# A hybrid RWKV-7, GLA and RetNet trunk: TensorE's order in the mixers taken from a model of the other engines' queues

## The chip, the cores and the metric

The kernel runs on one core of a Trainium2 chip. The metric is the device time of one execution in microseconds (us). Three runs of the kernel before took 3447.75, 3429.0 and 3440.02 us, a median of 3440.02. TensorE (PE in the profile) multiplies matrices, VectorE (DVE) and ScalarE (ACT) work on what it leaves in PSUM, GpSimd (POOL) works on SBUF, and SyncE (SP) issues most transfers. Each engine takes its instructions strictly in the order of the program and waits where an operand isn't ready.

## The reference

The reference is one inference step of two layers over 1024 new prompt tokens and 8 sample sequences of 4 tokens, width 1024, in float32. Each layer projects its input, runs three kinds of heads on parts of the projection, projects their output back, and applies a gated feed-forward network (FFN) with a short convolution:

```python
for l in range(DEPTH):
    p = x @ w_in[l]
    p_rw, p_gl, p_rt = _split(p, (RWKV_COLS, GLA_COLS, RET_COLS))
    y_a, sh, s_a = _rwkv7_mix(p_rw, ...)     # 6 heads
    y_b, s_b = _gla_mix(p_gl, ...)           # 5 heads
    y_c, s_c = _ret_mix(p_rt, s_ret[l], pos) # 5 heads
    mix = jnp.concatenate([y_a, y_b, y_c], axis=-1) @ w_out[l]
    x = _layer_norm(ALPHA * x + mix, ln1_g[l], ln1_b[l])
    f, cv = _conv_ffn(x, s_conv[l], ffn_up[l], ...)
    x = _layer_norm(ALPHA * x + f, ln2_g[l], ln2_b[l])

def step(s, inp):                            # RWKV-7, for each token
    r_t, w_t, a_t, b_t, k_t, v_t = inp
    sa = jnp.einsum('bhvk,bhk->bhv', s, a_t)
    s = s * w_t[:, :, None, :] + sa[..., None] * b_t[:, :, None, :] + v_t[..., None] * k_t[:, :, None, :]
    return s, jnp.einsum('bhvk,bhk->bhv', s, r_t)
```

GLA and RetNet are computed in chunks of 64 tokens with a state of their own. All final states are outputs too.

## The kernel before, in words

Large products keep float32 accuracy by splitting each operand into a high and a low part: `mm3` issues three matmuls, high times high, low times high and high times low. Their tiles are named `pa` (RWKV's part of the projection, channels by tokens), `gt` (the rest of the projection, tokens by channels), `po` (output projection), `pu` and `pd` (FFN). Weights come from DRAM by SyncE, and ScalarE (`wih`) and GpSimd or VectorE (`wil`) split them (L188).

The mixers of a layer run in two stages. In the first, RWKV works on nine batches, eight of 128 prompt tokens (two chunks of 64) and one of the samples. Of a batch, `rwkv_front` (L473) makes the operands with VectorE, ScalarE and GpSimd from two small products `zw` and `za`, up to `ra` and `bk` (L533); `rwkv_gram` (L537) multiplies them to gram matrices (`gps`, masked into `gm` at L559); `rwkv_solve` (L599) sends those through DRAM, solves a triangular system by pairs of VectorE instructions (L630, L632), and sends the result back. `rwkv_merge` (L647) joins the halves by the small products `xps`, `tps` and `ups`, each of which needs ScalarE's copy of the one before (L656, L661, L666); `rwkv_gate` makes the output gate (`gp`), in the same PSUM bank. `rwkv_core` (L678) runs one chunk: products with the state (`zy<-st`) and with the values (`zy<-sav`), ScalarE's copy `zs` (L688), the product `sp`, the copy `sav` (L693), the state update `up` with VectorE's L720, and the last products into `zy`, copied to `ys` (L698). In the second stage GLA (`gtp`, `gsp`, `gop`, `gup`) and RetNet (`rtp`, `rsp`, `rop`, `rup`) go through nine token tiles; `finish` (L979) normalizes a tile with a reduction (L985), a reciprocal root by Newton steps of tiny VectorE instructions (tiles `nw`, L242 to L248) and two products (L989, L990) into `yt`. `yrows` transposes `yt` (`ytp`), and `out_proj` multiplies by the output weights and adds the residual (`ac`, L1325) ahead of the layer norm (L940).

What sets TensorE's order is a small scheduler that runs while the program is written. Each part is a generator (`Stream`, L75) that emits a burst of instructions and then yields a time in us, an event or a condition. `Tensor.run` (L142) always steps the first stream whose time has come; the projection `gt` and `pa` serve as filler when no chain step is ready. `Tensor.order` (L111) adds to the clock `max(0.025, cols*passes/2400)` us for each matmul and chains every matmul to its predecessor, so TensorE keeps exactly this order. How long a step waits for its answer comes from the table `AFTER` (L35) of fixed delays, one number per kind of step. `TE.post` (L133) puts off a store or another action by such a number. The other engines' instructions stand in the order in which the streams emit them, as the tile framework places them.

Of the kernel before, what the change touches and what calls it, by code (L numbers as in the profile page):

```python
# [34 lines left out]
# expected times (us) from a step to what it makes ready  # L35
AFTER = {"key": 5.93, "sh": 3.5, "rkv": 2.0, "block": 6.0, "blockin": 2.5, "x": 3.0, "operands": 8.0, "gram": 0.9, "tv": 0.9, "tb": 0.9, "solve": 24.0, "ud": 4.5, "joined": 4.0, "mask": 1.5, "gd": 4.5, "x11": 1.28, "x21": 1.4, "x22": 0.6, "z": 1.4, "s": 1.58, "am": 2.0, "sx": 1.0, "sout": 3.0, "y": 7.3, "gate": 1.4, "state": 2.5, "done": 7.0, "turn": 2.5, "tokin": 3.36, "ev": 2.25, "gexp": 2.6, "gqt": 1.6, "rrot": 5.5, "rqt": 2.0, "at": 2.5, "qm": 0.8, "vx": 0.9, "gstate": 1.2, "tk": 4.5, "gateout": 4.0, "yin": 2.2, "yout": 4.5, "gnext": 1.2, "rout": 8, "rnext": 0.8, "yt": 0.5, "yready": 1.79, "ln": 3.0, "lnk": 1.5, "lns": 3.0, "ln1": 3.0, "ln2": 9.0}
# [18 lines left out]
# constant columns  # L55
# [9 lines left out]

class Event:
    """A time on the tensor engine from which something it has to wait for is expected."""

    def set(self, after=0.0):
        self.time = Event.clock() + after  # L70
# [4 lines left out]
class Stream:  # L75
    """Work on the tensor engine in bursts: yields the time (us) until the next one can start, or an Event or a condition."""
# [13 lines left out]
    def step(self, clock):  # L90
        x = next(self.gen, self)
        if x is self:
            return False
        if isinstance(x, (int, float)):
            self.ready = clock() + x
        else:
            self.wait = x
        return True


class Tensor:
    """The tensor engine, its instructions kept in the order of the program, with an estimate of its time (us)."""

    def __init__(self, tc, engine):
        self.tc, self.engine, self.t, self.last, self.posts = tc, engine, 0.0, None, []
# [5 lines left out]
    def order(self, ins, cols, passes):  # L111
# [5 lines left out]
        self.t += max(0.025, cols * passes / 2400)  # L117
# [1558 lines left out]
```

## Time and profile before

| | us |
|---|---|
| median of three runs | 3440.02 |
| span of the profiled execution (the page gives no other time of it) | 3430.9 |
| mixers of layer 0 | 0 to 929 |
| FFN of layer 0 | 929 to about 1718 |
| mixers of layer 1 | about 1718 to 2645 |
| FFN of layer 1 | 2645 to 3431 |

The profile has 22110 matmul instructions on TensorE, 5037 instructions on VectorE, 3208 on ScalarE and 1660 on GpSimd. The boundaries of the stages are read from the first `pu` and the first `pa` of the layers. In the waits of the profile a row names the engine and line that waits, the one waited for, then the sum, the number of times and the longest wait. Beside the busy times stands the clock that TensorE was granted, as a share of its full one.

### The profile page before, as it was taken

The page shows a single profiled execution, that of the slowest core. Times are in us where ns is not written, and L with a number is a line of the kernel's source. Part 1 is how long each engine was busy: PE and PEld are TensorE (multiplying, and loading weights), DVE is VectorE, ACT ScalarE, POOL GpSimd, SP SyncE. Part 2 cuts the span into 40 slices and gives each one's busy share as a digit, 9 for nine tenths or more (in the row PEclk, how much of TensorE's full clock was granted, in tenths as well). Part 3 has the DMA queues.
Part 4 walks back from the last instruction along what each step waited for, and adds up shares of the span by engine and source line. Part 5 has one row for each costly group of instructions (what it writes and reads, how often), then busy time and mean ns, then how long its engine had stood idle before and what let it go on. Part 6 is the DMA issues. An engine that isn't in the chain of part 4 may idle for free.

```text
span 3430.9 us, 59397 instructions
## 1 busy us (share of the span) xinstructions
PE 3198.4 (93%) x22110; PEld 2975.9 (87%) x22110; DVE 2068.6 (60%) x5037; ACT 1434.7 (42%) x3208; POOL 1332.6 (39%) x1660
## 2 busy tenths in 40 slices
PE   9889999988899999999888999999788999999995
PEld 8778888776799999999877888887777999999995
DVE  3577565776756544454746866646777564545457
ACT  6554332334543334333575543323346423333335
POOL 5443222224553334333565522221336433433345
PEclk9789999998999999999998999999989999999998
DMA  7333213433311111111154432234433111111111
GB/s 249 112 110 99 79 54 102 139 115 102 106 60 47 44 44 50 50 44 50 56 164 140 133 91 68 63 128 119 129 94 100 48 44 44 56 44 44 44 44 56
DMA packets 233261, 288.24 MB, mean 84 GB/s; under 512 B 65212, under 2 KB 146908, under 8 KB 232972
## 3 DMA queue, kind: packets, MB, share of 16 engines
q1 hardware_dynamic: 223852, 271.98, 26.3%
q10 hardware_dynamic: 9120, 12.47, 1.2%
q8 instruction: 173, 2.83, 0.4%
q14 instruction: 116, 0.95, 0.1%
HBM read 225.94 MB, written 58.43 MB: 83 GB/s over the span
## 4 chain that ended last, share of the span: by engine, by line
PE 70%; DVE 16%; DMA 4%; ACT 4%; issue 3%; POOL 2%; SPq 1%; ACTq 0%; DVEq 0%; POOLq 0%
PE pu L128 27%; PE pd L128 13%; PE gt L128 9%; PE pa L128 5%; PE po L128 3%; DVE tm L630 2%; DVE U L632 2%; PE zy L128 2%; PE gps L128 2%; PE rop L128 1%; DVE c L1401 1%; PE gop L128 1%; POOL wil L188 1%; DMA N<-gd 1%; DVE s L940 1%
## 5 line engine op out<-in xcount | busy, mean ns | idle before, releaser
L1401 DVE SCALAR_TENSOR_TENSOR c<-u,ppt,c 128x32 f32<-128x32 f32 (+1 forms) x704 | 395.8, 589 | 545.5 <-ACT c L1392 523.8
L188 POOL TENSOR_TENSOR wil<-wir,wih 128x512 fp32r<-128x512 f32 (+1 forms) x264 | 366.3, 1395 | 365.8 <-ACT wih L188 361.2
L128 PE MATMUL gt<-wih,xh 128*128 128x320 f32 (+1 forms) x1008 | 340.1, 339 | 0.9 <-DVE mx L388 0.9
L1448 DVE TENSOR_TENSOR acc<-acc,pd 128x384 f32<-128x384 f32 (+1 forms) x480 | 247.7, 518 | 139.5 <-PE pd L128 137.5
L128 PE MATMUL gt<-wil,xh 128*128 128x320 f32 (+1 forms) x1008 | 316.1, 315 | 6.5 <-POOL wil L188 5.2
L128 PE MATMUL gt<-wih,xl 128*128 128x320 f32 x896 | 281.6, 314 | 0.0
L188 ACT CAST wih<-wir 128x512 fp32r<-128x512 f32 (+1 forms) x296 | 185.6, 637 | 162.4 <-PE po L128 71.5
L128 PE MATMUL pa<-xh,wih 128*128 128x384 f32 (+1 forms) x576 | 216.5, 376 | 20.4 <-DVE mx L388 11.8
L630 DVE TENSOR_TENSOR tm<-U,N 96x60 f32<-96x60 f32 (+24 forms) x558 | 179.1, 321 | 69.9 <-DMA N<-gd 48.4
L128 PEld LDWEIGHTS gt<-wih,xh 128*128 128x128 f32 (+1 forms) x1008 | 187.5, 186 | 38.6 <-issue 21.9
L128 PE MATMUL pa<-xl,wih 128*128 128x384 f32 (+1 forms) x576 | 201.4, 350 | 3.3 <-POOL xl L188 3.0
L128 PE MATMUL pa<-xh,wil 128*128 128x384 f32 (+1 forms) x576 | 200.7, 348 | 3.6 <-POOL wil L188 2.2
L128 PEld LDWEIGHTS gt<-wil,xh 128*128 128x128 f32 (+1 forms) x1008 | 188.5, 187 | 10.2 <-POOL wil L188 9.1
L188 POOL TENSOR_TENSOR hl<-c,hh 128x384 fp32r<-128x384 f32 x132 | 128.1, 971 | 159.6 <-ACT hh L188 133.0
L632 DVE TENSOR_TENSOR U<-U,tm 96x60 f32<-96x60 f32 (+24 forms) x558 | 170.3, 305 | 14.0
L128 PEld LDWEIGHTS gt<-wih,xl 128*128 128x128 f32 x896 | 173.1, 193 | 0.0
L1392 ACT ACTIVATE c<-pu,ppt 128x384 f32<-128x384 f32 (+1 forms) x264 | 172.8, 655 | 0.0
L1380 ACT COPY u<-pu 128x384 f32<-128x384 f32 x176 | 84.1, 478 | 195.2 <-PE pu L128 195.1
L188 ACT CAST hh<-c 128x384 fp32r<-128x384 f32 x132 | 64.4, 488 | 222.4 <-DVE c L1407 222.3
L128 PEld LDWEIGHTS pa<-xh,wih 128*128 128x128 f32 x576 | 119.7, 208 | 35.1 <-DVE mx L388 13.2
L128 PE MATMUL po<-yh,wih 128*128 128x384 f32 (+1 forms) x384 | 138.9, 362 | 9.1 <-DVE ac L1325 6.7
L128 PE MATMUL po<-yh,wil 128*128 128x384 f32 (+1 forms) x384 | 131.7, 343 | 3.7 <-DVE wil L188 3.7
(810 smaller groups left out, 9862.6 us busy)
## 6 DMA issues: line engine op xcount, KB each, us to landing
wir<-in_wA_dram SPq DMA_DIRECT2D x144, 256.0 KB
wir<-in_wO_dram SPq DMA_DIRECT2D x96, 256.0 KB
wir<-in_wB_dram SPq DMA_DIRECT2D x56, 320.0 KB
tokd<-ev SPq DMA_DIRECT2D x112, 160.0 KB
x<-rkvd SPq DMA_DIRECT2D x16, 576.0 KB
tk<-tokd SPq DMA_DIRECT2D x16, 480.0 KB
rkvd<-mx SPq DMA_DIRECT2D x36, 192.0 KB
tk<-tokd SPq DMA_DIRECT2D x16, 400.0 KB
```

The lines of the kernel that those rows point to most:

```text
L128: self.order(self.engine.matmul(out, lhsT, rhs, start=start, stop=stop), cols, 4 if rhs.dtype == F32 else 1)
L188: return A.copy(dst_h, src), (le or G).tensor_tensor(dst_l, src, dst_h.bitcast(F32), ALU.subtract)
L630: V.tensor_tensor(tm, U[:, 0:nr, i:i + 1].to_broadcast([4 * ns, nr, 31 - i]), N[:, i:i + 1, i + 1:32].to_broadcast([4 * ns, nr, 31 - i]), ...
L632: V.tensor_tensor(U[:, 0:nr, i + 1:32], U[:, 0:nr, i + 1:32], tm, ALU.add)
L940: self.ends["V"] = V.tensor_tensor(self.s1, acc[0] if k == 1 else self.s1, acc[k], ALU.add)
L1380: A.copy(u[:, 2:386], ps)
L1392: A.activation(c[:, :W], ps, AF.Identity, scale=pc(PP_CV + 4 * t + 2), bias=pc(PP_CV + 4 * t + 3))
L1401: V.scalar_tensor_tensor(cv, src, pc(PP_CV + 4 * t + tap), cv, ALU.mult, ALU.add)
L1448: V.tensor_tensor(acc[n][m], acc[n][m], ps, ALU.add)
```

## The change

The table `AFTER` goes, but for three constants. In its place a `Model` is kept while the program is written: a list of busy intervals for VectorE, ScalarE, GpSimd and SyncE's queue, the time at which each region of a tile is written and last read, and a single figure for the transfers' bus. Every instruction of those engines is wrapped (`Timed`): it is entered into its engine's list at the first gap from the time its operands and its buffer are ready, with a cost by its size. TensorE's clock is raised to the time at which the model has the operands of a matmul ready. `ready(x)` is the modelled time at which `x` can be read, and `slot(tag)` of a pool the time at which its next buffer is free. Every `yield AFTER[...]` becomes a yield of such times, and every post fires at such a time. The projection's steps also wait for their weights and for a free bank, in the model. The chain's `turn` delay is left out. What is computed and the number of instructions on each engine stay as they are, save ScalarE's table loads: the program has 71 where it had 65.

```diff
-AFTER = {"key": 5.93, ..., "x": 3.0, "operands": 8.0, "gram": 0.9, ..., "x11": 1.28, "x21": 1.4, "x22": 0.6, "z": 1.4, "s": 1.58, ..., "gate": 1.4, "state": 2.5, "done": 7.0, "turn": 2.5, ..., "yt": 0.5, "yready": 1.79, ...}
+PACE = {"x": 3.0, "start": 4.0, "lnk": 1.5}
...
+class Model:
+    TABLE = {AF.Exp: "e", AF.Tanh: "e", AF.Ln: "l", AF.Gelu_apprx_tanh: "g"}
...
+    def ready(self, *aps):
+        t = 0.0
+        for ap in aps:
+            n, r = self.box(ap)
+            t = max(t, self.latest(self.writes.get(n, {}), r))
+        return At(t)
...
+    def place(self, e, at, dur):
+        b = self.busy[e]
+        i = len(b)
+        while i > 1 and b[i - 1][0] >= at:
+            i -= 1
+        while True:
+            t = max(at, b[i - 1][1])
+            if i == len(b) or t + dur <= b[i][0]:
+                b.insert(i, (t, t + dur))
...
+    def cost(self, e, op, out, ins, func):
...
+        if e == "V":
...
+                o = m / 960 + 0.065
+            return o, o + 0.15
+        if e == "A":
+            o = m / 1200 + 0.055
+            return o, o + 0.15
...
+        o = m * 2.34 / 1000 + 0.06
+        return o, o + 0.1
...
-        self.t += max(0.025, cols * passes / 2400)
+        self.t = self.model.matmul(out, lhsT, rhs, self.t, dur) + dur
...
+        dur = 2 * max(0.03, cols * 2 / 2400 + 0.006) if rhs.dtype == F32 else cols / 2400 + 0.0135
...
             A.copy(x11[0:32], ps[0:32, :384])
-            yield AFTER["x11"]
+            yield ready(x11[0:32])
...
-            yield AFTER["x22"]
+            yield ready(s.sh[0], s.sh[1])
             rwkv_gate(s)
...
             A.copy(zs, zy[Cn:C2, :w])
-            yield AFTER["z"]
+            yield ready(zs)
...
             A.copy(savc[0:Cn], sp[:Cn, :w])
-            yield AFTER["s"]
+            yield ready(savc[0:Cn])
...
-                yield AFTER["gate"]
+                yield late(ready(s.gm, s.sav), 0.0 if s.smp else ready(sts[state_at[0]]), pz.slot("zy"))
...
                         if c:
-                            yield AFTER["state"]
+                            yield late(ready(sts[state_at[0]]), pz.slot("zy"))
...
-                s.done.set(AFTER["done"])
-                yield AFTER["turn"]
+                s.done.set()
...
-            yield AFTER["x"]
+            yield late(ready(s.sh[0]), pm.slot("m", ahead=2))
...
-            yield AFTER["operands"]
+            yield ready(s.ra, s.bk)
...
+                    yield late(pg.slot("g"), feed.at(2 * 3 * NA + 4 * gi, 0))
                     ps = pg.tile([P, 512], F32, tag="g", name="gt")
...
-                s.out.set(AFTER["rout"])
-                yield AFTER["rnext"]
+                s.out.set(ready(s.yt))
+                yield pn.slot("b", BB)
...
-                    yield AFTER["yt"]
+                    yield pg.slot("g")
                 if i % 3 == 2:
-                    yready[n].set(AFTER["yready"])
+                    yready[n].set(ready(*ys[n][:2]))
```

How the order moves is shown at three places. The rows have the line, the operation, the tile written and the tiles read, the shape, and how often a row repeats. All matmuls of the changed kernel carry the line of its helper, L322, and all its VectorE instructions that of the wrapper, L253.

First TensorE, layer 0, the merge and the first chunk of a batch in the middle of the stage. Before, from `ups` to the chunk's product with the state:

```order
L128 MATMUL ups<-gm,x_3579 32x32 x12
L128 MATMUL tv<-cs,v 128x128 x3
L128 MATMUL gp<-bgt,sh 128x384
L128 MATMUL gp<-bgt,sg 128x384
L131 MATMUL tb<-cs,bk 128x128 x4
L128 MATMUL gt<-wih_2999,xh_401 128x320
L128 MATMUL gt<-wil_2998,xh_401 128x320
L128 MATMUL gt<-wih_2999,xl_402 128x320
L128 MATMUL gt<-wih_2999,xh_401 128x320
L128 MATMUL gt<-wil_2998,xh_401 128x320
L128 MATMUL gt<-wih_2999,xl_402 128x320
L128 MATMUL zy<-st_165,ra 128x128 x3
```

and in the changed kernel, from `ups` to `sp`:

```order
L322 MATMUL ups<-gm,x_3847 32x32 x12
L322 MATMUL gp<-bgt,sh 128x384
L322 MATMUL gp<-bgt,sg 128x384
L322 MATMUL zy<-st_165,ra 128x128 x3
L322 MATMUL zy<-sav,gm 64x64 x6
L322 MATMUL gt<-wih_3616,xh_92 128x320
L322 MATMUL gt<-wil_3615,xh_92 128x320
L322 MATMUL gt<-wih_3616,xl_93 128x320
L322 MATMUL gt<-wih_3616,xh_92 128x320
L322 MATMUL gt<-wil_3615,xh_92 128x320
L322 MATMUL gt<-wih_3616,xl_93 128x320
L322 MATMUL sp<-zs,gm 64x64 x6
```

`gp` and `zy` follow `ups` directly, and six products of `gt` stand ahead of `sp`; `tv` and `tb` of another batch have moved elsewhere.

Second TensorE, layer 0, the gram matrices of the first batch. Before:

```order
L128 MATMUL gps<-ra,bk 128x128 x4
L128 MATMUL pa_1_1084<-xh_222,wih_1009 128x384
L128 MATMUL pa_1_1084<-xl_223,wih_1009 128x384
L128 MATMUL pa_1_1084<-xh_222,wil_1008 128x384
L128 MATMUL pa_1_1084<-xh_222,wih_1009 128x384
L128 MATMUL pa_1_1084<-xl_223,wih_1009 128x384
L128 MATMUL pa_1_1084<-xh_222,wil_1008 128x384
L128 MATMUL gps<-ra,bk 128x128 x4
```

and in the changed kernel:

```order
L322 MATMUL gps<-ra,bk 128x128 x8
L322 MATMUL pa_1_1238<-xh_172,wih_1149 128x384
L322 MATMUL pa_1_1238<-xl_173,wih_1149 128x384
L322 MATMUL pa_1_1238<-xh_172,wil_1148 128x384
L322 MATMUL gps<-ra,bk 128x128 x2
L322 MATMUL pa_1_1238<-xh_172,wih_1149 128x384
L322 MATMUL pa_1_1238<-xl_173,wih_1149 128x384
L322 MATMUL pa_1_1238<-xh_172,wil_1148 128x384
L322 MATMUL gps<-ra,bk 128x128 x2
L322 MATMUL tv<-cs,v 128x128 x3
```

Eight products of `gps` come in a row where two groups of four had six large products between them.

Third VectorE, layer 0, second stage, the end of a RetNet tile's normalization. Before (the `nw` with the higher numbers belong to GLA's tile, whose output is `yg`):

```order
L246 TENSOR_TENSOR nw_7867<-nw_7866 128x5
L248 SCALAR_TENSOR_TENSOR nw_7895<-nw_7896,nw_7895 128x5
L247 SCALAR_TENSOR_TENSOR nw_7867<-nw_7867,nw_7865 128x5
L1029 TENSOR_TENSOR tk<-tk,E 128x320
L246 TENSOR_TENSOR nw_7896<-nw_7895 128x5
L248 SCALAR_TENSOR_TENSOR nw_7866<-nw_7867,nw_7866 128x5
L247 SCALAR_TENSOR_TENSOR nw_7896<-nw_7896,nw_7894 128x5
L989 TENSOR_TENSOR yt<-yt,nw_7866 128x320
L248 SCALAR_TENSOR_TENSOR nw_7895<-nw_7896,nw_7895 128x5
L1089 TENSOR_TENSOR qm<-qT,cs 128x256
L990 SCALAR_TENSOR_TENSOR yt<-yt,gate 128x320
```

and in the changed kernel:

```order
L253 SCALAR_TENSOR_TENSOR nw_8106<-nw_8107,nw_8106 128x5
L253 TENSOR_TENSOR nw_8107<-nw_8106 128x5
L253 SCALAR_TENSOR_TENSOR nw_8107<-nw_8107,nw_8105 128x5
L253 SCALAR_TENSOR_TENSOR nw_8106<-nw_8107,nw_8106 128x5
L253 TENSOR_TENSOR nw_8107<-nw_8106 128x5
L253 SCALAR_TENSOR_TENSOR nw_8107<-nw_8107,nw_8105 128x5
L253 SCALAR_TENSOR_TENSOR nw_8106<-nw_8107,nw_8106 128x5
L253 TENSOR_TENSOR yt<-yt,nw_8106 128x320
L253 TENSOR_TENSOR yl_8185<-ytp,yh_8184 128x4x128
L253 SCALAR_TENSOR_TENSOR yt<-yt,gate 128x320
```

One normalization runs at a time: GLA's tiles have gone through theirs before RetNet's first `yt`.

More of the change, by code (lines that the diff above doesn't have):

```diff
@@ L64, with set @@
 NCS = _off
+class At(float):
+    pass
 class Event:
-    def set(self, after=0.0):
-        self.time = Event.clock() + after
+    def set(self, at=0.0):
+        self.time = max(Event.clock(), at)
     time = None
@@ new lines, with __init__, __getattr__, traced @@
+class Timed:
+    def __init__(self, model, engine, name):
+        self.model, self.engine, self.name = model, engine, name
+    def __getattr__(self, op):
+        call = getattr(self.engine, op)
+        def traced(*args, **kw):
+            ins = call(*args, **kw)
+            aps = [a for a in list(args) + list(kw.values()) if isinstance(a, bass.AP)]
+            func = next((a for a in args if isinstance(a, AF)), None)
+            self.model.add(self.name, op, ins, aps[0], aps[1:], func)
+            return ins
+        return traced
@@ new lines, with __init__, tile, slot @@
+class Pool:
+    def __init__(self, model, pool, bufs, since):
+        self.model, self.pool, self.bufs, self.since, self.tags = model, pool, bufs, since, {}
+    def tile(self, shape, dtype, tag=None, name=None, bufs=None, **kw):
+        key = tag or name
+        if tag is not None:
+            kw["tag"] = tag
+        if bufs is not None:
+            kw["bufs"] = bufs
+        t = self.pool.tile(shape, dtype, name=name, **kw)
+        n = t.tensor.name
+        h = self.tags.setdefault(key, [])
+        b = bufs or self.bufs
+        if len(h) >= b:
+            self.model.before[n] = h[-b]
+        elif self.since:
+            self.model.floor[n] = self.since
+        h.append(n)
+        return t
+    def slot(self, tag, bufs=None, ahead=1):
+        h, b = self.tags.get(tag, []), bufs or self.bufs
+        return At(max([self.model.idle(n) for n in h[len(h) - b:len(h) - b + ahead] if len(h) >= b] or [self.since]))
@@ L101, with late, __init__ @@
+def late(*times):
+    return At(max(times))
 class Tensor:
-    def __init__(self, tc, engine):
-        self.tc, self.engine, self.t, self.last, self.posts = tc, engine, 0.0, None, []
+    def __init__(self, tc, engine, model):
+        self.tc, self.engine, self.model, self.t, self.last, self.posts = tc, engine, model, 0.0, None, []
         Event.clock = self.clock
@@ L109, in clock, with order @@
         return self.t
-    def order(self, ins, cols, passes):
+    def order(self, ins, out, lhsT, rhs, dur):
         ins = ins.ins
@@ L270, in gemm_steps @@
     def gemm_steps(feed, first, xs, n, name, free):
+        yield late(pg.slot("g"), feed.at(first, 0), ready(xs[n][0][:, 0], xs[n][1][:, 0]))
         ps = pg.tile([P, 512], F32, tag="g", name=name)[:, :NB[n][1]]
@@ L274, in gemm_steps @@
         for k in range(KD):
+            if k:
+                yield late(feed.at(first, k), ready(xh[:, k], xl[:, k]))
             h, lo, end = feed.k(first, k)
@@ L568, in rwkv_tok @@
             s.vt = rp.tile([P, 384], F32, tag="vt", name="vt", bufs=2)[:W]
+            yield late(ready(s.v), pm.slot("m"))
             tv = pmt("tv")
@@ L1326, in out_proj @@
                 ln.add(m, V if n == 2 else G)
-            yield AFTER["ln"]
+            yield late(ready(ln.s1, ln.s2), pg.slot("g", ahead=2))
             ln.stats()
```

333 lines of the change are left out of this document (221 added, 112 removed).

## The prediction

> **What bounds the kernel now.** I read the page first, for the engine that sets the end, then busy time by stage, then TensorE's waits, then the granted clock in short windows.
>
> ```profile
> span 3430.9 us, 59397 instructions
> ...
> PE 70%; DVE 16%; DMA 4%; ACT 4%; issue 3%; POOL 2%; SPq 1%; ACTq 0%; DVEq 0%; POOLq 0%
> ```
>
> TensorE is the bound, with 70% of the chain that ended last, and VectorE is the only other engine with a large share of it. The same by stage (first column the stretch, then its length, then busy time and instructions of each engine; the decimal ahead of the last two numbers is TensorE's mean granted clock):
>
> ```profile
> 0.00:275.00 275.00, 242.48 (x1476) 218.64 (x1477) 156.55 (x423) 158.13 (x330) 135.63 (x158) 0.85 0.51 156
> 275.00:605.00 330.00, 317.09 (x2714) 277.97 (x2713) 198.72 (x745) 112.35 (x272) 82.65 (x80) 0.97 0.29 84
> 605.00:929.00 324.00, 277.39 (x2104) 234.05 (x2103) 239.16 (x561) 133.17 (x344) 115.71 (x95) 0.92 0.39 116
> ...
> 1718.00:1975.00 257.00, 226.73 (x1473) 202.76 (x1471) 160.97 (x451) 166.83 (x356) 144.45 (x166) 0.90 0.50 147
> 1975.00:2310.00 335.00, 319.67 (x2796) 280.18 (x2797) 206.08 (x758) 115.36 (x288) 85.16 (x85) 0.98 0.31 87
> 2310.00:2645.00 335.00, 287.60 (x2119) 245.84 (x2119) 241.82 (x570) 144.90 (x355) 121.06 (x107) 0.92 0.36 108
> ```
>
> The rows are the two layers' mixers, three stretches each; the FFNs, left out here, have the same order on TensorE in both programs. So the change can act on these 1856 us. Length less PE busy leaves 32.5, 12.9, 46.6, 30.3, 15.3 and 47.4, or 185 us, without work on TensorE. One minus the clock, times the length, gives 41, 10, 26, 26, 7 and 27, or 136 us, that the clock took. What TensorE waited for:
>
> ```profile
> PE ytp L131 <- DVE yt L990: 20.2, 10, 4.0
> PE ytp L131 <- DVE ac L1325: 18.0, 5, 7.2
> ...
> PE gps L128 <- DVE bk L533: 12.5, 5, 6.0
> ...
> PE zy L128 <- ACT ys L698: 4.2, 2, 2.4
> PE zy L128 <- DVE st L720: 3.2, 1, 3.2
> PE sp L128 <- ACT zs L688: 2.6, 3, 1.6
> PE up L128 <- ACT sav L693: 2.4, 2, 1.8
> PE gp L128 <- ACT gm L666: 1.8, 1, 1.8
> ```
>
> The last five rows are the handovers inside the RWKV chain: 14.2 us in all. The fixed delays cover the chain well already; the transposes of the mixers' output (ytp), 38.2 us, are the largest item.
>
> **The change, part by part.** The work is the same; its order on TensorE differs, and with it the cover, the work that lies between a product and the product that waits for another engine's answer.
>
> *The chain's steps.* Between two steps stood twelve products of gt or pa, now six, and between ups and gp none (the order of the fifth batch shows it). What an answer takes:
>
> ```profile
> 315.67 0.42 PE L128 MATMUL gt<-wih,xh 128*128 128x320 f32 x1
> ...
> 315.92 0.31 PE L128 MATMUL gt<-wil,xh 128*128 128x320 f32 x1
> ...
> 316.07 0.31 PE L128 MATMUL gt<-wih,xl 128*128 128x320 f32 x1
> ...
> 345.12 1.32 PE L128 MATMUL zy<-sav,gm 64*64 64x64 f32 x12
> 348.07 0.48 ACT L688 COPY zs<-zy 64x384 f32<-64x384 f32 x1
> 349.41 0.91 PE L128 MATMUL sp<-zs,gm 64*64 64x64 f32 x12
> 350.36 0.47 ACT L693 COPY sav<-sp 64x384 f32<-64x384 f32 x1 [0.20 <-PE sp L128]
> ```
>
> Products of gt follow each other 0.15 us apart at full clock, so six products give some 0.88 us of cover. sp ends at 350.32 and its copy at 350.83: 0.51 us, covered still. zy ends at 346.44 and its copy only at 348.55, since ScalarE was busy: 2.11 us, which leaves a wait of 1.23 us behind 0.88. How often ScalarE is free shows in its own waits for these products:
>
> ```profile
> ACT zs L688 <- PE zy L128: 60.8, 25, 7.2
> ACT sav L693 <- PE sp L128: 27.4, 25, 2.4
> ACT gm L666 <- PE ups L128: 27.0, 15, 3.7
> ACT x L661 <- PE tps L128: 18.4, 12, 3.8
> ACT x L656 <- PE xps L128: 12.3, 8, 3.0
> ```
>
> It stood ready 85 times of 116 (34 zs, 34 sav, 16 of each other); 31 were late, and at 1.23 us each the cost is at most 38 us, at least nothing, as the model holds ScalarE's queue. I take a third, **+13**. gp now comes right behind ups and needs its bank, which a copy of 0.468 us (the row of gm below) frees: 16 times 0.55 us with its handover, **+9** (0 to 9: no other work stands there to hide it).
>
> ```profile
> L666 ACT COPY gm<-ups x16: 468/468/472, 188.0 to 2208.5; 32x384 f32<-32x384 f32 x16
> 314.08 1.80 DVE L720 SCALAR_TENSOR_TENSOR st<-up,pt,st 64x64 f32<-64x64 f32 x6 [6.73 <-PE up L128]
> ```
>
> The new state takes 1.80 us behind up. Before a batch's second chunk the cover falls from 3.5 us and more to about 1.7, so 0.1 to 0.4 us is missing where VectorE is free and more where it isn't: **+7** for 16 places (0 to 24).
>
> *The fronts.* gps of the first two batches of a layer comes with less cover after its lora product za (8.8 to 7.3 us, and 9 to 6.2, counted in products), and those are where the gps row above waits up to 6.0. Twice (1.5 + 2.8) is **+9** (0 to 9).
>
> *The finish.* ytp stands 7.3 us of work behind its rop, where it stood 11.1. But VectorE's queue between the reduction L985 and the last operation on yt falls from 36 instructions to 21 in the tiles that used to overlap GLA's: the second chain of nw is gone from between (third pair of the order), and with it rows that wait for TensorE, such as GLA's qm and sg.
>
> ```profile
> 321.47 0.17 DVE L247 SCALAR_TENSOR_TENSOR nw<-nw,nw 128x6 f32<-128x6 f32 x1
> 321.67 0.17 DVE L248 SCALAR_TENSOR_TENSOR nw<-nw,nw 128x6 f32<-128x6 f32 x1
> ```
>
> These small steps follow 0.20 us apart, so 15 fewer are 3.0 us at least; at the mean of that stage, 239.16/561 = 0.43 us, they are 6.4. Against 3.8 less cover the answer comes between 0.8 later and 2.6 earlier, and the ten yt waits are 2.0 each. I take it near the upper end, since the rows that waited for TensorE go: the yt row vanishes, the ac row stays, **-20** (+8 to -38).
>
> *The clock.* Windows of the chip's clock, PE busy, then the clock:
>
> ```profile
> 96.20:116.70 20.50, 17.33 (x56) 0.50 0.42 118
> 1843.90:1867.80 23.90, 19.57 (x64) 0.50 0.31 95
> 341.98:345.39 3.41, 1.64 (x10) 1.00 0.33 83
> 345.39:348.80 3.41, 3.41 (x20) 0.50 0.33 126
> ```
>
> A window with 1.77 us of idle time is followed by one at half clock. The first two rows are the first and the last of five long half-clock stretches (20.5, 20.5, 17.1, 17.1 and 23.9 us, 99.1 together), which hold alternations such as four gps, six pa, four gps. Now the gps come eight in a row, with runs of 24 large products behind, longer than a window of 3.41 us. If the five end a half sooner, 50 us pass at full instead of half clock, and 25 are saved; a few short ones go with the ytp waits. I take **-30**. At best the five vanish, -50; at worst the new waits start a dozen stretches of one window, +20.
>
> [...]
>
> *Switches.*
>
> ```profile
> L423 ACT ACT_TABLE_LOAD x18 | 23.1, 1283 | 0.3
> ```
>
> TensorE's order has 2014 runs of equal work where it had 2093; at 0.1 us a switch (the first gt product above, behind gps, shows 0.42 us, the next 0.31) **-8** (0 to -8). Six more table loads on ScalarE, 65 to 71, at 1283 ns are 7.7 us of its time, which the stage rows leave idle for 90 us and more in every stage: hidden, at most +7.7. SP's and POOL's instructions are the same in number; their stores go out when the model has the tile ready.
>
> **Sum:** 13 + 9 + 7 + 9 - 20 - 30 - 8 = -20 us, so a span of 3410.9. The page gives the profiled execution's span alone; the median of the three runs shown, 3440.02, lies 9.1 us above it. Forecast: **3420 us**.
>
> **The rivals.** *Nothing moves.* The ytp waits are VectorE's backlog in a stage where it is busy 239.16 of 324 us; another order on TensorE only shifts where they are met. Without the 20 the sum is 0: **3440 us**. For it speaks that GLA's and RetNet's rows of the trace have the most idle time and the lowest density; against it that VectorE still idles a quarter there.
>
> *Tight bursts lose the clock (slower).* The steps xps to the second zy now follow one another with 0.88 us of work between them. If two steps of one 3.41-us window each wait 0.65 us, the window has 1.3 us of idle time, near the 1.77 behind which half clock was seen. One such window in each of 16 batches costs 1.7 us each, 27 us, and the late copies at their upper end 25 more: 3420 + 52 = **3472 us**. For it: the copies are late in 31 of 116 cases; against it: 85 found ScalarE free, and those 0.88 us cover.
>
> *The model's VectorE is too fast (slower).*
>
> ```profile
> 122.86 1.28 POOL L188 TENSOR_TENSOR wil<-wir,wih 128x512 fp32r<-128x512 f32 x1
> 122.98 1.21 DVE L630 TENSOR_TENSOR tm<-U,N 96x29 f32<-96x29 f32 x1
> 125.19 0.18 DVE L630 TENSOR_TENSOR tm<-U,N 96x28 f32<-96x28 f32 x1
> ```
>
> A step of the solve takes 1.21 us beside a POOL subtraction and 0.18 alone, and the model charges no such thing. If three such meetings put each of the 16 batches 3 us late where the covers are now cut to fit, it is 48 us: **3468 us**. Against it: the first gps waited 6.0 behind a cover of 8.8, so its answer took some 15 us, and in the later batches the new order leaves it 15 to 20.
>
> [...]
>
> **How the numbers follow.** Forecast 0.44, nothing moves 0.25, tight bursts 0.21, VectorE too fast 0.10. A difference of 0.5%, 17 us, is about what a measurement of this kernel can tell from none. So faster 0.44, same 0.25, slower 0.31. The forecast's own range is 3395 to 3423. The bounds of its terms reach down to 3420 - 13 - 9 - 20 = 3378, with the copies, the fronts and the clock at their good ends, and up to the rivals at 3472; with half the spread of the runs, (3447.75 - 3429.0)/2 = 9, on either side that is 3369 to 3481.
>
> **What would show it.** Right: the ytp rows by DVE yt nearly gone, fewer half-clock stretches above 10 us, the six mixer stretches at some 1836 us together. The chain's cost shows in the waits sp for zs, up for sav, gp for gm, zy for st: about 30 us more together. Wrong: those rows above 60 us or a clock under 0.95 in 275 to 605 (tight bursts); gps waiting for bk in later batches (VectorE); ytp unchanged (nothing moves). The FFNs must stay within a few us.

## The result and the profile after

The changed kernel takes 3598.74 us (median of 4 runs, 3592.62 to 3603.3), the kernel before 3440.1. The ratio is 1.047, with a 95% interval of 1.044 to 1.050: slower by some 160 us where 20 us less were forecast, and outside the range.

The same stages as before, of the changed kernel (the first three rows and the fifth to seventh are the mixers of the two layers, the fourth and the last the FFNs; the columns are those of the table in the prediction):

```profile
0.00:256.00 256.00, 213.97 (x1304) 195.18 (x1305) 135.65 (x358) 155.85 (x319) 136.25 (x156) 0.86 0.54 165
256.00:609.00 353.00, 330.68 (x2692) 283.99 (x2691) 206.08 (x809) 112.31 (x271) 77.07 (x79) 0.85 0.25 72
609.00:1000.00 391.00, 316.32 (x2300) 273.51 (x2299) 242.08 (x564) 140.95 (x357) 121.27 (x100) 0.87 0.33 104
1000.00:1776.00 776.00, 768.01 (x4760) 764.53 (x4760) 423.61 (x751) 296.52 (x625) 315.51 (x486) 0.99 0.15 48
1776.00:2062.00 286.00, 235.36 (x1467) 210.10 (x1465) 170.01 (x429) 179.46 (x373) 152.92 (x173) 0.83 0.46 137
2062.00:2405.00 343.00, 312.78 (x2457) 266.90 (x2457) 201.45 (x777) 106.18 (x256) 78.26 (x78) 0.82 0.25 71
2405.00:2795.00 390.00, 327.76 (x2378) 283.38 (x2377) 239.75 (x563) 143.18 (x360) 120.29 (x99) 0.89 0.34 106
2795.00:3601.50 806.50, 770.35 (x4766) 766.39 (x4765) 441.52 (x790) 317.03 (x657) 331.32 (x493) 0.98 0.15 48
```

The FFNs kept their clock, 0.99 and 0.98. The boundaries here are the first `pu` and the first `pa` of each layer. Read from the same rows, those of before are 929, 1705 and 2624 us; the table ahead of the prediction has 1718 and 2645, which lie inside layer 1's mixers and its FFN. So the mixers took 1848 us and now take 2019, while the FFNs stayed at 776 and 807. In the steady part of RWKV's stage (second and sixth row) the clock is 0.85 and 0.82, where it was 0.97 and 0.98. Over the whole span:

```profile
core 0: 3430.9 us, clock 0.952
```

before, and after

```profile
core 0: 3601.5 us, clock 0.913
```

One minus the clock, times the span, is the time that TensorE's clock withheld: 165 us before, 313 after, 149 more before rounding. Not all of that is time lost, for the clock is low in waits too, where no product runs: 5.86 us of the first stretch of 37.50 below. What the 171 us of the span are made of stands in the busy times of the two pages, before and after:

```profile
PE 3198.4 (93%) x22110; PEld 2975.9 (87%) x22110; DVE 2068.6 (60%) x5037; ACT 1434.7 (42%) x3208; POOL 1332.6 (39%) x1660
```

```profile
PE 3275.2 (91%) x22110; PEld 3044.0 (85%) x22110; DVE 2060.2 (57%) x5037; ACT 1451.5 (40%) x3214; POOL 1332.9 (37%) x1660
```

The same 22110 matmuls kept TensorE busy 77 us longer, at the lower clock. The span less this busy time, TensorE's idle time, went from 232.5 to 326.3 us, 94 more. So the loss has two parts, a lower clock on the same work and more waiting, and the waiting is the larger. TensorE's waits in the changed kernel:

```profile
PE ytp L325 <- DVE yt L253: 73.0, 15, 13.4
PE gps L322 <- DVE bk L253: 27.3, 4, 11.2
...
PE tps L322 <- ACT x L253: 19.3, 7, 8.3
PE gp L322 <- ACT gm L253: 18.6, 16, 3.1
...
PE ups L322 <- ACT x L253: 10.0, 5, 4.2
...
PE up L322 <- ACT sav L253: 1.7, 3, 0.6
...
PE sp L322 <- ACT zs L253: 1.2, 2, 0.6
```

ytp and gps wait longer, and gp waits for each of its 16 banks. The row of ytp for ac, 18.0 us before, is gone, so ytp's waits went from 40.5 to 76.4 in all (with 2.3 and 3.4 for yl). The two waits of the chunks (zs, sav) did not grow. Four of the long stretches of half clock, between 184 and 369 us (length, PE busy, clock), and the merge inside the second one:

```profile
184.20:221.70 37.50, 31.64 (x209) 0.50 0.25 70
249.00:276.30 27.30, 20.22 (x131) 0.50 0.35 90
303.60:320.70 17.10, 15.20 (x76) 0.50 0.20 54
354.80:368.50 13.70, 12.38 (x61) 0.50 0.24 62
```

```profile
254.81 1.49 PE L322 MATMUL tps<-x,gm 32*32 32x32 f32 x24 [8.27 <-ACT x L253]
...
258.91 1.48 PE L322 MATMUL ups<-gm,x 32*32 32x32 f32 x24 [0.71 <-ACT x L253]
260.95 1.65 PE L322 MATMUL gp<-bgt,sh 128*128 128x384 f32 x2 [0.56 <-ACT gm L253]
```

Here a burst of the chain follows a wait of 8.27 us, and the whole burst then runs at half clock: 1.49 us for the 24 records of tps that took 0.94 before.

### The profile page after: what moved, and what is told of

Same layout as the page of the kernel before. It is cut to its first block, busy times and chain, and to the rows that moved or that the text cites. A ratio compares the mean times of both kernels' runs of the same rounds, so it can differ in the third digit from the quotient of the medians.

```text
span 3601.5 us, 59486 instructions
## 1 busy us (share of the span) xinstructions
PE 3275.2 (91%) x22110; PEld 3044.0 (85%) x22110; DVE 2060.2 (57%) x5037; ACT 1451.5 (40%) x3214; POOL 1332.9 (37%) x1660
## 5 line engine op out<-in xcount | busy, mean ns | idle before, releaser
L253 DVE SCALAR_TENSOR_TENSOR c<-u,ppt,c 128x32 f32<-128x32 f32 (+1 forms) x704 | 396.5, 590 | 544.9 <-ACT c L253 523.3
L253 POOL TENSOR_TENSOR wil<-wir,wih 128x512 fp32r<-128x512 f32 (+1 forms) x264 | 367.0, 1400 | 459.9 <-ACT wih L253 431.4
L322 PE MATMUL gt<-wih,xh 128*128 128x320 f32 (+1 forms) x1008 | 357.7, 356 | 0.0
L322 PE MATMUL gt<-wil,xh 128*128 128x320 f32 (+1 forms) x1008 | 332.3, 331 | 8.0 <-POOL wil L253 7.7
L253 DVE TENSOR_TENSOR acc<-acc,pd 128x384 f32<-128x384 f32 (+1 forms) x480 | 247.6, 517 | 139.4 <-PE pd L322 137.5
L322 PE MATMUL gt<-wih,xl 128*128 128x320 f32 x896 | 292.8, 327 | 0.0
L253 ACT CAST wih<-wir 128x512 fp32r<-128x512 f32 (+1 forms) x296 | 184.6, 637 | 161.3 <-PE po L322 71.2
L322 PEld LDWEIGHTS gt<-wih,xh 128*128 128x128 f32 (+1 forms) x1008 | 199.2, 198 | 27.5 <-issue 12.4
L253 DVE TENSOR_TENSOR tm<-U,N 96x60 f32<-96x60 f32 (+24 forms) x558 | 161.3, 289 | 104.4 <-DMA N<-gd 85.7
L322 PE MATMUL pa<-xh,wih 128*128 128x384 f32 (+1 forms) x576 | 208.7, 362 | 13.2 <-ACT wih L253 7.3
L322 PEld LDWEIGHTS gt<-wil,xh 128*128 128x128 f32 (+1 forms) x1008 | 201.5, 200 | 13.5 <-POOL wil L253 11.9
L253 ACT COPY u<-pu 128x32 f32<-128x32 f32 (+1 forms) x352 | 124.3, 379 | 196.8 <-PE pu L322 195.8
L322 PE MATMUL pa<-xh,wil 128*128 128x384 f32 (+1 forms) x576 | 196.8, 342 | 4.3 <-POOL wil L253 4.1
L322 PE MATMUL pa<-xl,wih 128*128 128x384 f32 (+1 forms) x576 | 197.9, 344 | 2.5 <-POOL xl L253 2.2
L253 POOL TENSOR_TENSOR hl<-c,hh 128x384 fp32r<-128x384 f32 x132 | 128.3, 972 | 161.3 <-ACT hh L253 134.7
L322 PEld LDWEIGHTS gt<-wih,xl 128*128 128x128 f32 x896 | 183.7, 205 | 0.0
L253 ACT ACTIVATE c<-pu,ppt 128x384 f32<-128x384 f32 (+1 forms) x264 | 172.9, 655 | 0.0
L253 DVE TENSOR_TENSOR U<-U,tm 96x60 f32<-96x60 f32 (+24 forms) x558 | 161.3, 289 | 15.3
L253 ACT CAST hh<-c 128x384 fp32r<-128x384 f32 x132 | 64.4, 488 | 221.8 <-DVE c L253 221.6
L322 PE MATMUL po<-yh,wih 128*128 128x384 f32 (+1 forms) x384 | 140.3, 365 | 10.6 <-DVE ac L253 10.6
L253 POOL COPY u<-u 128x2 f32<-128x2 f32 x176 | 40.3, 230 | 285.2 <-ACT u L253 230.5
L322 PEld LDWEIGHTS pa<-xh,wih 128*128 128x128 f32 x576 | 118.2, 205 | 23.9 <-ACT wih L253 8.1
```

The lines of the kernel that those rows point to most:

```text
L253: ins = call(*args, **kw)
L322: self.order(self.engine.matmul(out, lhsT, rhs, start=start, stop=stop), out, lhsT, rhs, dur)
```

## The experiments

Theory A: the close order of small products makes TensorE lose its clock. Theory B: RetNet's finish, left alone at the end of the mixers, is the loss. "Floors" below are the old fixed delays kept as least delays beside the modelled times.

**1. Delays put back in the changed kernel.** In the first (e1), at the chain:

```diff
-            yield ready(zs)
+            yield AFTER["z"]
...
-                yield late(ready(s.gm, s.sav), 0.0 if s.smp else ready(sts[state_at[0]]), pz.slot("zy"))
+                yield AFTER["gate"]
```

> The changed kernel with the fixed delays of before put back at the steps of the RWKV chain alone (merge, gate, core, second chunk, turn). Theory A (bunched chain steps lose TensorE's clock): the clock between the first gt and the first gtp comes back from 0.85 and 0.82 to 0.93 or more, and the time falls by 40 to 90 us from 3599, to 3510 to 3560. Theory B (the loss is RetNet's part left alone at the end, behind a VectorE that GpSimd blocks): the time stays within 15 us of 3599. Theory C (the gps clusters cost the clock): the clock stays below 0.9 in that stretch.

In the second (e2) the same kind of edit at every step of GLA, RetNet, ytp and the layer norm:

```diff
-                s.out.set(ready(s.yt))
-                yield pn.slot("b", BB)
+                s.out.set(TE.t + AFTER["rout"])
+                yield AFTER["rnext"]
```

> The changed kernel with the fixed delays of before put back at the steps of GLA, RetNet, the transposes and the layer norm alone. Theory B: the stretch from the first gtp to the first pu falls from 391 us towards 340 in each layer, the time by 60 to 120 us, to 3480 to 3540. Theory A alone: the time stays within 15 us of 3599.

In the third (e3) both, with the output projection waiting until its weights are ordered, which its place in the new order asks for:

> Both sets of fixed delays put back; fronts, grams, token products, stores and the projection's waits stay with the model. Theories A and B together: 3430 to 3470, within 1% of the kernel before. If the rest of the change (fronts, projection's waits) has a part of the loss: 3480 to 3540.

Measured: 3552.24 us (ratio to before 1.0343, 1.0322 to 1.0364), 3567.01 (1.0387, 1.0371 to 1.0402) and 3505.33 (1.0200, 1.0167 to 1.0234). The chain gives 46 back, the second stage 32, both together 93. A and B each hold a part, and 69 us lay elsewhere. In e1 the time fell as A had it, but the clock of RWKV's stage came back only to 0.88 and 0.91, not to 0.93; TensorE's busy time fell by 51 us and its idle time by 1. In e2 the time came out between the two ranges. With the front, gram and token delays put back as well (e5),

```diff
-                        yield pm.slot("m")
+                        yield AFTER["gram"]
```

> As e3_both_delays, and the fixed delays of before also at the fronts, the gram matrices and the token products of RWKV; stores, solve and the projection's waits stay with the model. Theory D (what is left of the loss, 69 us, comes from the eight gps in a row and the token products without work between): 3440 to 3465. Theory E (it comes from the projection's waits and the posts at modelled times): within 15 us of 3505.

it was 3600.61 us, which neither theory had. Fixed delays beside a clock that the model moves make another order, neither that of before nor that of the change, so this kind of edit is no clean test; the floors of experiment 4 are.

**2. Parts of the change, alone, in the kernel before.** Only numbers of `AFTER` are edited (in e9 also the order of actions that are due at the same time). First the chain's (e4):

```diff
-"x11": 1.28, "x21": 1.4, "x22": 0.6, "z": 1.4, "s": 1.58, ..., "gate": 1.4, "state": 2.5, ..., "turn": 2.5
+"x11": 0.6, "x21": 0.6, "x22": 0.0, "z": 0.7, "s": 0.7, ..., "gate": 0.0, "state": 1.3, ..., "turn": 0.0
```

> The kernel before with the chain's delays alone cut to about the free answer of ScalarE (x11 and x21 0.6, x22 0, z and s 0.7, gate 0, state 1.3, turn 0). Theory A: the clock between the first gt and the first gtp falls from 0.97 to below 0.92 and the time rises by 30 us or more, to 3470 to 3530. Rival (the copies are covered at 0.88 us, the chain's spacing costs nothing): within 15 us of 3440.

3568.66 us, ratio 1.0389 (1.0371 to 1.0407), 132 us more than the 3436.37 beside it. The steady part of RWKV in layer 0 and 1 of this kernel:

```profile
303.80:604.70 300.90, 282.72 (x2281) 241.25 (x2279) 177.62 (x704) 95.34 (x228) 65.70 (x67) 0.87 0.24 71
...
2074.20:2372.60 298.40, 277.58 (x2202) 235.19 (x2201) 173.49 (x662) 93.51 (x223) 63.35 (x66) 0.86 0.24 68
```

0.87 and 0.86, near the 0.85 and 0.82 of the changed kernel, by eight numbers and with no model. TensorE is busy 107 us longer and idle 34 us longer, so this part of the loss is mostly clock. Theory A stands for the chain; the rival that the spacing costs nothing falls. The merge's three numbers alone (e9), then the others alone (e10):

> The kernel before with the delays of the merge alone cut (x11 and x21 0.6, x22 0; two actions due at the same time now keep their order). Theory A1 (the 32x32 products of the merge, which lost the clock in the probe though nothing waited, cost it when they stand close): most of the 132 us of e4, 60 to 110 us more than before. Theory A2 (idle time in the chunks' steps costs the clock): under 40 us.

> The kernel before with the delays of the chunks alone cut (z and s 0.7, gate 0, state 1.3, turn 0). Theory A1: under 50 us more than before. Theory A2: 80 to 130 us more.

3484.98 us (1.0138, 1.0111 to 1.0164) and 3514.13 (1.0224, 1.0203 to 1.0245), beside 3438.06: 47 and 76 us, which add up to nearly the 132. Each theory expected one of them to hold most, and both missed: merge and chunks share the loss.

Then gram, tv and tb at 0.0, so that the gram products stand together (e6):

> The kernel before with the delays of gram, tv and tb at zero, so that the gps and the token products of a batch stand together, everything else as it was. Theory D: the clock in the RWKV stage falls and the time rises by 15 us or more. The prediction's own step (alternation costs the clock, clusters spare it): the long half-clock stretches get shorter and the time falls by 10 to 30 us.

3477.07 us, 1.0132 (1.0102 to 1.0161). The prediction had put clusters down as sparing the clock; this edit costs 43 us. It is no copy of the change's clusters, though, for each group waits until VectorE has masked one before it, 23.7 us in all, where the kernel before waited 2.7 and the changed kernel 0.2:

```profile
PE gps L128 <- DVE gm L559: 23.7, 20, 4.3
```

So part of the 43 us is this wait, and what the change's own clusters of gps cost was not tested apart. Chain and clusters together (e12):

> The kernel before with both the chain's delays of e4_tight_before and the gram and token delays of e6_gram_clusters. If bunching on TensorE is the cause of the whole loss: 132 + 43, so 3590 to 3625, as the changed kernel. If the two overlap: 3570 to 3585.

3647.89 us, 1.0605 (1.0577 to 1.0633): 210 us, more than the sum of 175 and above both ranges.

Longer delays instead (e8: x11 and x21 2.2, x22 1.5, z 2.3, s 2.5, gate 2.3, state 3.5):

> The kernel before with the chain's delays made longer (x11 and x21 2.2, x22 1.5, z 2.3, s 2.5, gate 2.3, state 3.5). Theory A: fewer half-clock stretches between the first gt and the first gtp, the same time or up to 20 us less. Against: the chain ends later and pushes GLA and RetNet back, 10 to 40 us more.

3453.9 us, 1.0056 (1.0036 to 1.0075): 20 us more, as the second range had it. The clock between the first gt and the first gtp did rise, to 0.98 and 0.99, as Theory A said, but over the whole span it was 0.940 against 0.952. And gram at 1.6, tv and tb at 1.4 (e16):

> The kernel before with gram at 1.6 and tv and tb at 1.4 in place of 0.9, so that more large products stand between the gram and the token products. Theory A: fewer half-clock stretches in the front of a layer, 5 to 25 us below before. If the chip already holds the clock there or the solve comes later: within 10 us of before or above.

3445.35 us, 1.0025 (1.0008 to 1.0042). The old spacing is near its best; wider is not better.

**3. The clock by itself.** Probes stand between tiles of the dense FFN of layer 0 and add work of their own, so only their windows count, not the time. In the first kernel (e7):

```diff
+                for i in range(20):
+                    for h in range(6):
+                        TE.matmul(ps[0:64, h * 64:h * 64 + 64], cs[0:64, 0:64], pt[:, h * 64:h * 64 + 64], start=True, stop=True)
+                    A.copy(pt, ps[0:64, 0:384])
+                    for d in range({13: 3, 16: 6, 19: 12}[j]):
+                        TE.matmul(pb_[:, 0:320], w[d % 8][d // 8 % 2], xh[:, d % 8, 0:320], start=True, stop=True)
```

> The kernel before with six probes put into the FFN of layer 0, ahead of its tiles 4, 7, 10, 13, 16 and 19: 300 products of 32x32, 160 of 64x64 and 100 of 128x128, each by themselves with nothing to wait for; then three times twenty steps of six 64x64 products, a copy by ScalarE that the next step needs, and 3, 6 or 12 large products beside the copy. Theory A1 (small products count little for the clock, busy or not): the gapless bursts of 32x32 and 64x64 fall to half clock, and so do the steps with 3 and perhaps 6 large products, not those with 12. Theory A2 (only idle time counts): the gapless bursts keep the full clock, the steps with 3 lose it by their gap of about 0.3 us each, those with 6 and 12 keep it.

Each of the two kernels of probes ran once. Length, PE busy and clock: 32x32 products alone (two rows), 64x64 alone, 128x128 alone, then the steps with 3 large products (two rows: the first 5.5 us, then the rest) and with 6:

```profile
1068.60:1073.30 4.70, 4.70 (x150) 1.00 0.26 85
1073.30:1097.30 24.00, 24.00 (x456) 0.50 0.01 3
1191.20:1210.00 18.80, 18.80 (x321) 1.00 0.10 31
1325.30:1347.60 22.30, 22.30 (x203) 1.00 0.06 18
1439.90:1445.40 5.50, 3.68 (x42) 1.00 0.30 95
1445.40:1490.10 44.70, 44.70 (x263) 0.50 0.00 1
1606.90:1645.00 38.10, 38.10 (x361) 1.00 0.03 11
```

Products of 32x32, without any wait, lost the clock after 4.7 us; those of 64x64 and 128x128 kept it, over 18.8 and 22.3 us, so A1 holds for the merge's shape only. The sixth row shows a second thing: TensorE is busy the whole 44.7 us and the clock does not come back. The wait, 1.82 us, lay in the first 5.5 us of this probe. The steps with 6 large products had no wait at all (1.00 over 38.1 us). Those with 12 had one of 0.56 us and kept the clock (1.00 over 56.3 us), so this wait did not cost it. The second kernel of probes (e11):

> The kernel before with six other probes in the FFN of layer 0, twenty steps each: twelve 32x32 products, a copy that the next step needs, and 3, 6 or 12 large products beside it (tiles 4, 7, 10); twelve 32x32 products and 6 large ones with nothing to wait for (13); six 64x64 and 3 large with nothing to wait for (16); six 64x64, two copies one after the other and 6 large ones, so that some 0.3 us of each step are idle (19). Theory A1: half clock in 4, 7 and 13, and not in 16; Theory A2: none in 13 and 16, half clock in 4 and 19.

Here 32x32 steps with a copy and 3 large products (the first 10.2 us, then the last 29.3), with 6 (two rows: the first 4.5 us, then the rest, and below them two rows of the large products that follow the probe), with 12, then 32x32 with 6 and 64x64 with 3 that wait for nothing, and last 64x64 with two copies and 6, behind its first wait:

```profile
1066.60:1076.80 10.20, 10.20 (x188) 1.00 0.12 40
1080.20:1109.50 29.30, 29.30 (x319) 0.50 0.00 1
1203.00:1207.50 4.50, 2.67 (x52) 1.00 0.39 113
1207.50:1268.90 61.40, 61.40 (x554) 0.50 0.01 2
1269.20:1272.40 3.20, 3.20 (x12) 0.50 0.00 0
1272.40:1275.80 3.40, 3.40 (x21) 1.00 0.00 0
1385.90:1442.10 56.20, 56.20 (x721) 1.00 0.03 9
1534.40:1573.00 38.60, 38.60 (x601) 1.00 0.05 16
1688.40:1717.70 29.30, 29.30 (x300) 1.00 0.04 15
1815.10:1876.70 61.60, 61.60 (x330) 0.50 0.00 1
```

The same work of twelve 32x32 and six large products takes 38.6 us without a wait and 65.9 with 1.83 us of idle time in the first 4.5: less than 2 us of waiting cost 27 in all. But the first two rows have no idle time, and the clock fell all the same: twelve 32x32 products with three large ones lost it some 11 us after their start. So in the probes the clock was lost in two ways: behind a short wait at the start of mixed small and large products (1.83 us in 4.5, 1.82 in 5.5), and without a wait where twelve 32x32 products had three large ones between them (as with 32x32 alone). In both the steps then ran at half clock without any idle time (61.4 and 44.7 us behind the waits, the last 29.3 of the steps without one), and behind the 61.4 the clock was back after 3.2 us of large products alone. Neither theory had both: A1 expected half clock in tile 13, which kept it, and A2 expected it from waits alone, of which tile 4 had none.

In the changed kernel both ways can be seen. Of its 58 stretches of half clock, the shortest of 3.41 us, 50 start behind 3.41 us that hold more than 1 us of idle time. The other eight, 119 us of 631, start behind less; one of them is this, behind the 32x32 products of xps and the small zw and za:

```profile
2266.30:2269.70 3.40, 3.40 (x50) 1.00 0.58 182
2269.70:2290.20 20.50, 19.94 (x131) 0.50 0.03 9
```

How much of the 77 us each of the two ways makes was not tested.

**4. Floors in the changed kernel.** All modelled times stay:

```diff
-            yield ready(zs)
+            yield late(ready(zs), TE.t + AFTER["z"])
...
-                        yield pm.slot("m")
+                        yield late(pm.slot("m"), TE.t + AFTER["gram"])
```

at the chain, the gram and the token products (e13):

> The changed kernel with every modelled time kept, and the fixed delays of before as least delays beside them at the RWKV chain, the gram matrices and the token products (the output projection also waits until its weights are ordered). Theory A (bunching in RWKV is nearly all of the 160 us): 3440 to 3480. If the order of GLA and RetNet has a loss of its own: 3490 to 3550, with the stretch from the first gtp to the first pu above 350 us in each layer.

at GLA, RetNet, their finish and ytp too (e14):

> As e13, with least delays also at GLA, RetNet, their finish and the transposes. Theory A: within 15 us of e13. If the RetNet finish has a loss of its own (ytp waits 76 us in the changed kernel): 30 to 60 us below e13, and the ytp waits below 45 us.

and last (e18)

```diff
-            yield ready(s.ra, s.bk)
+            yield late(ready(s.ra, s.bk), TE.t + 14.0)
```

> As e14_floors_all, and the gram products at least 14 us behind the front's lora products. If the fronts are the larger part of the 80 us that are left: 3460 to 3495, with gps waits below 12 us. If what is left is spread over the order: within 15 us of 3520.

3539.96 us (1.0301, 1.0278 to 1.0325), 3519.94 (1.0250, 1.0226 to 1.0274) and 3441.09 (1.0024, 1.0007 to 1.0040). In this sequence RWKV's spacing gives 59 us, the second stage 20, and the front 79: with all three the changed kernel is back at the time of before. I had expected RWKV to hold nearly all, so theory A as worded missed, in e13 and e14; the front was the largest part, and e18 came out below the 3460 that I had as the lowest. Its floor of 14 us is longer than the 8.0 of before, though, and the same 14 us make the kernel before 18 us faster (experiment 5); like for like, 24 us of the loss are left. In e13 the clock of RWKV's stage is back at 0.94 and 0.95. TensorE's waits without the floor at the front and with it:

```profile
PE gps L323 <- DVE bk L254: 28.1, 4, 12.2
PE ytp L326 <- DVE yt L254: 27.2, 8, 4.9
```

```profile
PE ytp L326 <- DVE yt L254: 31.9, 9, 6.4
...
PE gps L323 <- DVE gm L254: 9.5, 4, 3.8
```

The wait for bk, 28.1 us, is gone. TensorE's idle time fell by 52 us in all and its busy time by 29, at a clock of 0.946 in place of 0.930. The first pair of rows also answers B: ytp fell from 73.0 to 27.2 us, and the floors that did it were worth 20.

One number of the model itself (e15), what VectorE and ScalarE write being seen 1.0 us after its cost:

```diff
-            return o, o + 0.15
+            return o, o + 1.0
```

> The changed kernel with one number changed: what VectorE and ScalarE write is seen 1.0 us after their cost in place of 0.15. It widens the cover of every step by 0.85 us, some six large products. If the model's thin covers are the fault: 40 to 110 us below the changed kernel's 3599. If the order of phases is: within 20 us.

3584.61 us (1.0429, 1.0400 to 1.0459): 14 us less. The clock is 0.902, lower than in the changed kernel. That is within the 20 us expected if the order of phases is the fault: thicker covers alone don't mend it. The waits did shrink at ytp (8.6 us) while the clock got worse. What makes it worse there stays open.

**5. A version that beats both.** The kernel before, one number (e17):

```diff
-"operands": 8.0
+"operands": 14.0
```

> The kernel before with one number changed: operands 14.0 in place of 8.0, so that the gram products come when bk is there. The gps waits, 12.5 us, and the half-clock stretches of 20.5 us behind them at 96 and 141 should go: 10 to 30 us below before. If the later gram products only make the solve and the chain late: 0 to 20 us above.

3417.54 us, ratio 0.9947 (0.9929 to 0.9965), 18 us less than the 3435.41 beside it. At the place of the first stretch of 20.5 us (0.50 before):

```profile
94.00:118.00 24.00, 21.45 (x126) 1.00 0.67 199
```

The gram products come when bk is there, none of them waits for it any more, and the clock stays up. Around the second stretch of 20.5 us, at 141, it is still 0.69.

**All kernels together.** Busy and idle are TensorE's, from the page of each kernel; time withheld is one minus the mean clock, times the span. The last four columns are differences to the kernel before, in us:

| kernel | span, us | clock | more span | more busy | more idle | more withheld |
|---|---|---|---|---|---|---|
| before | 3430.9 | 0.952 | | | | |
| after | 3601.5 | 0.913 | +171 | +77 | +94 | +149 |
| e1 delays, chain | 3549.8 | 0.926 | +119 | +26 | +93 | +98 |
| e2 delays, second stage | 3571.1 | 0.919 | +140 | +66 | +75 | +125 |
| e3 delays, both | 3511.1 | 0.930 | +80 | +32 | +48 | +81 |
| e5 delays, fronts too | 3599.2 | 0.916 | +168 | +88 | +80 | +138 |
| e4 tight chain | 3571.5 | 0.916 | +141 | +107 | +34 | +135 |
| e9 tight merge | 3492.5 | 0.937 | +62 | +54 | +8 | +55 |
| e10 tight chunks | 3512.3 | 0.932 | +81 | +55 | +26 | +74 |
| e6 clusters | 3474.4 | 0.939 | +44 | +25 | +18 | +47 |
| e12 tight chain and clusters | 3646.8 | 0.904 | +216 | +124 | +92 | +185 |
| e8 wide chain | 3441.0 | 0.940 | +10 | +18 | -8 | +42 |
| e16 wide gram | 3440.4 | 0.952 | +10 | -5 | +14 | +0 |
| e13 floors in RWKV | 3540.4 | 0.927 | +110 | +37 | +73 | +94 |
| e14 floors | 3518.5 | 0.930 | +88 | +35 | +52 | +82 |
| e18 floors, front | 3437.9 | 0.946 | +7 | +7 | +0 | +21 |
| e15 slow model | 3584.6 | 0.902 | +154 | +83 | +71 | +187 |
| e17 before, front | 3415.7 | 0.958 | -15 | -19 | +4 | -21 |

Busy and idle add up to the span. The withheld time follows it within some 35 us, but it counts half clock in waits too, so it can't be set against the span as its cause. By these columns the chain's spacing costs clock: its tight form adds 107 us of busy time (e4), and putting the delays back into the changed kernel takes 51 off the busy time and 1 off the idle time (e1). The floors of the second stage take off idle time alone, 21 us (e13 to e14), and that of the front 52 us of idle and 29 of busy time (e14 to e18).

## Why the prediction was wrong, by its own steps

- **What bounds the kernel**: right. TensorE is the bound, only the mixers moved, the FFNs stayed within 1 us. The two boundaries that were read wrong, 1718 and 2645, shift its stage rows by 13 and 21 us; no term of the sum hangs on them.
- **The clock, -30**: this is the step that failed first, in its sign. The same matmuls kept TensorE busy 77 us longer, against a stated worst of +20. Its argument was that alternating small and large products cost the clock and clusters spare it, drawn from stretches such as that of the gram products. The runs show that the chain's closer steps cost it (0.916 in e4, where 0.952 was; the other way 0.926 in e1, from 0.913), and the probes show two ways: behind 1.83 us of waiting in mixed work 61.4 us ran at half clock, and twelve 32x32 products with three large ones between them lost the clock without a wait, some 11 us after their start. Alternation that waited for nothing kept the full clock where six large products stood beside twelve of 32x32 (38.6 us), or three beside six of 64x64 (29.3 us). e6 speaks against the gram clusters as well, but has waits of its own.
- **The waits, +18 in all** (13 + 9 + 7 + 9 - 20): the second step that failed. TensorE's idle time grew by 94 us. The largest piece is the finish (below); others had no term, such as zp, which waited 11.3 us for mx, bp 11.2 for its transfer and tv 7.9 for gm, all without a row before.
- **The chain's steps, +13, +9 and +7**: the waits for the merge's copies (tps and ups) grew by 12 us, from 16.3 and 0.8 to 19.3 and 10.0, those for zs and sav shrank by 2, and gp grew by 17 where 9 was its upper bound. The wait of zy for st, 3.2 before, has no row any more where +7 stood. That is 24 us of 29 as waits, but from other rows than those named. As time the spacing is worth 132 us in e4 and 59 with the floors (those of the gram and token products among them), at a clock of 0.916 in e4 against 0.952, and of 0.927 in e13 against 0.913.
- **The fronts, +9**: the wait grew by 15 us, from 12.5 to 27.3, and in e18 the place is worth 79 us, of which the kernel before could have had 18 too. The row of 6.0 us of wait and the row of 20.5 us at half clock behind it both stood in the prediction; they were never put into one price.
- **The finish, -20**: wrong in sign. ytp waits 73.0 us for yt where it waited 20.2, and 76.4 in all where it was 40.5. The half about VectorE held: from the end of a tile's last rop to the end of its yt it took 12.1 us, on the mean of the 18 tiles, where it took 15.0. But TensorE's work between that rop and the ytp that needs yt fell by more, from a median of 12.2 us to 7.1, where 3.8 less was reckoned. One tiny step beside GpSimd's work was slow:

```profile
819.84 4.72 DVE L253 TENSOR_SCALAR nw<-rsm 128x5 f32<-128x5 f32 x1
819.86 1.28 POOL L253 TENSOR_TENSOR wil<-wir,wih 128x512 fp32r<-128x512 f32 x1
821.10 0.99 POOL L253 TENSOR_TENSOR s<-s,sq 128x384 f32<-128x384 f32 x1
822.06 2.47 POOL L253 TENSOR_TENSOR wil<-wir,wih 128x512 fp32r<-128x512 f32 x2
```

  This step of 128x5 took 4.72 us beside four GpSimd instructions back to back, where the median of the 36 that write nw from rsm is 0.17. It does not make the growth of the waits, though, for the kernel before had such steps too (least, median and longest in ns):

```profile
L243 DVE TENSOR_SCALAR nw<-nw x54: 150/166/5069, 218.8 to 2561.0; 128x5 int32<-128x5 int32 x32, 128x6 int32<-128x6 int32 x16, 32x5 int32<-32x5 int32 x4, 32x6 int32<-32x6 int32 x2
```

  and all 648 steps into nw together took 164.0 us before and 152.1 after. So theory B has its wait, and the shorter cover fits as the cause of it; that was read from the traces and not tested apart.
- **Switches -8, table loads +0**: too small to be seen beside the rest.
- **The rivals**: "tight bursts lose the clock" was the nearest, at a chance of 0.21: its sign came, a clock of 0.85 in RWKV's stage where under 0.95 was named, and its size was the error. It was priced at one window of 3.41 us at half clock for each batch, 27 us; in the changed kernel the four stretches shown are 37.5, 27.3, 17.1 and 13.7 us long. The other term of it, 25 us of late copies, was not seen at zs and sav. "VectorE too fast" named the wait of gps for bk, which did grow, but in four places and not in every batch.
- **The idle time ahead of half clock**: the prediction had read 1.77 us of it in one window of 3.41. The probe agrees: half clock stood behind 1.83 us of idle time in 4.5. What the prediction did not weigh is how long the half clock then lasts, 61.4 us in that probe.

What stays open: why the slow model of e15 has the lowest clock of all, what the 24 us between e18 and e17 are, how much of the clock's loss comes from waits and how much from the 32x32 products, and what the change's own gram clusters cost.

## What to carry to other kernels

A model that starts each step as soon as its operands are ready packs the small products of a chain together and leaves no slack; the granted clock fell with it here, from 0.952 to 0.913. Keep large products between the steps as a floor, beside the model's times (a clock of 0.927 in e13). Split a loss into TensorE's busy and idle time before giving it to the clock. Price a wait inside mixed small and large products by the half-clock stretch behind it (61.4 us behind 1.83 in the probe), read from the clock in short windows, not by its own length. A place where a long half-clock stretch follows a single wait is worth trying with a later start: here one number, 6 us more before the gram products, gave 18 us.

## What the runs showed of the hardware that was not expected

- Products of 32x32 alone lost the clock after 4.7 us with TensorE busy all the time; 64x64 and 128x128 alone kept it for 18.8 and 22.3 us. Twelve of 32x32 with three large ones, with no idle time, lost it after some 11 us; with six large ones they kept it for 38.6 us.
- Half clock outlasted the wait ahead of it: 61.4 us without idle time behind 1.83 us of it, for work that kept the full clock over 38.6 us when nothing waited. Behind it, large products alone brought the clock back after 3.2 us.
- A VectorE instruction on 5 elements a partition took 4.72 us beside four GpSimd instructions back to back, where the median of its kind is 0.17; the kernel before had one of 5.07 us, again beside four.
